# Chunk sums, gate and squares of a Mamba-2 mixer kept in their PSUM banks, the sum of squares moved to VectorE

## The chip, the core and the metric

The kernel runs on one core of a Trainium2 chip: TensorE (PE) for matmuls, VectorE (DVE), ScalarE (ACT) and GpSimd (POOL) for elementwise work, SyncE (SP) for issuing transfers. TensorE writes into PSUM, which has eight banks of 128 partitions x 512 fp32 here; the other engines' data lies in SBUF. The metric is the time of one execution in microseconds on the device. Differences are ratios of times of the kernel before and after on the same chip.

## What is computed

One layer of a diffusion backbone: a bidirectional Mamba-2 mixer over 512 latent tokens, whose scans begin with the state that 256 context tokens leave, and then a convolutional gated MLP. All is fp32 at a model width of 1024, with 32 heads of 64 channels in four groups, states of 128, chunks of 128 tokens. Cut to what matters here:

```python
def ssd_chunked(xs, dt, a, bm, cm, init, with_output):
    ...
    cb = jnp.einsum("bclgn,bcsgn->bcgls", cc, bc)
    mix = cb[:, :, :, None] * jnp.exp(segsum(la))
    y = (jnp.einsum("bcgrls,bcsgrp->bclgrp", mix, xd)
         + jnp.einsum("bclgn,bcgrpn,bcgrl->bclgrp", cc, carried[:, :-1], jnp.exp(la_cs)))

def mamba2_output(y, xs, z, d, norm_w, w_out):
    y = (y.astype(z.dtype) + d * xs).reshape(bsz, l, SSM_INNER)
    return rmsnorm(y * jax.nn.silu(z), norm_w) @ w_out
...
x = x + g1 * ol
x = x + g2 * conv_ffn(modulate(rmsnorm(x, norm2_w[i]), sh2, sc2), ...)
return rmsnorm(x, final_norm_w)
```

`y` is summed over the two directions. For each chunk of a group it has three parts: within the chunk, from the forward state, and from the backward state.

## The kernel before

The features lie in the partitions, the tokens in the free dimension. `u` is an SBUF array of 16 tiles of 128 features x 512 tokens; it holds `xs` at first and is turned into the gated `y` in place. fp32 matmuls are made of three passes: a weight is split by `split` into a high part `hi` (a cast on ScalarE) and a rest `lo` (a subtraction on VectorE, some on GpSimd), and `mm3` adds hi x hi, lo x hi and hi x lo in one bank.

The mixer goes over four groups of heads (`ssm_group`), and within a group over four chunks. For a chunk, `mixing` makes the decay matrices: for each half of the heads and each direction a row `L` is loaded from DRAM, GpSimd writes a diagonal `dg`, VectorE scans `L`; GpSimd adds both directions and multiplies with `cb`. `mixing` also loads `eb`, the decays of the carried states (one buffer, 128 x 2 x 512, two transfers on SP's queue). Then, in lines 760 to 784: TensorE makes `pi`, the part within the chunk, and for each direction `pe`, the part of a carried state `S`. VectorE multiplies each `pe` by its half of `eb`, in SBUF, adds the halves, adds `d * u + pi` into `u` with four instructions on 128 x 128 (those with `d_col`), and adds the sum of the halves into `u`. `pi` and `pe` take turns in the three banks of the pool `py`. `advance` carries a state on: `weighted` (GpSimd's `xw`, ScalarE's `xh`, VectorE's `xl`), three matmuls into `ps_S`, a product on GpSimd and an addition on VectorE.

`gate_pieces` (lines 786 to 801) makes, for each of the 16 feature tiles `m`, the projection `pz` in one of the three banks of the pool `pj`, its Silu `sz` in SBUF on ScalarE, the product `u * sz` on VectorE, the square `sq` in SBUF on ScalarE, and on GpSimd the running sum `acc` of the squares (the first square goes straight into `acc`). `sz` and `sq` take slots of the three-slot SBUF tag `w2k`, which the convolutions `cv` use too. `acc` is later summed over the partitions by TensorE (`ssq`) for the mixer's norm.

`proj_pieces` (projections `pl`, `pc`, convolution and Silu of the next group), `gate_pieces` and `ada_pieces` (sums of the conditioning on VectorE, `ada_acc`) are the fill: `blend` strews it among the pieces of `ssm_group`, the next group's projections beside this group's chunks. That is the order of the program; the order on each engine is made when the program is built, by a scheduler that places instructions by its own reckoning of when buffers and operands come free. On the chip each engine takes its instructions in that order. After the mixer follow the output projection `o` in eight accumulators, three of which take over the banks of `pj`, and the MLP (`pa`, `pg`, `d`).

Nearly every instruction is recorded at line 58, the wrapper of the engines, so the views are read by tiles.

Of the kernel before, what the change touches and what calls it, by code (L numbers as in the profile page):

```python
# [39 lines left out]
# (exp(r) - 1) / r for |r| <= ln(2) / 2, and log(1 + u) / u for 0 <= u <= 1 in powers of u - 1/2  # L40
# [7 lines left out]
class Engine:  # L48
    """an engine whose instructions keep the order of the program while `held` is set"""
# [16 lines left out]
def hybrid_kernel(  # L66
# [21 lines left out]
    # ---------------------------------------------------------------- helpers  # L88
# [50 lines left out]
    def mean_part(p_, n, b):  # L139
        """p_ / n + b"""  # L140
        nb = small.tile([P, 1], F32, tag="rp_b", name="rp_b")
        V.scalar_tensor_tensor(nb, p_, 1.0 / n, eps_c if b is None else b, ALU.mult, ALU.add)
        return nb

    def rsqrt_pair(parts, n, b=None):
        """two factors per partition whose product is 1 / sqrt(sum(parts) / n + EPS); b is a mean_part"""
# [13 lines left out]
    # ---------------------------------------------------------------- constants  # L160
# [51 lines left out]
    # ---------------------------------------------------------------- conditioning  # L212
    def ada_mm(ps, k, w):
        """rows of s @ ada_w, partial sums in the partitions 32 j + (lat, ctx)"""
        j = k % 4
        mm(ps[32 * j:32 * j + 32, :], s_pad[:, k], w, start=(k < 4), stop=(k >= 4))
# [28 lines left out]
    def ada_load(q):  # L245
        """columns [256 q, 256 q + 256) of the shifts and of the scales"""
# [39 lines left out]
    def keep_busy(n, ps=junk):  # L286
        """the clock of the tensor engine falls while it waits"""
# [13 lines left out]
    def normalize(i, eng=V):  # L301
        """token blocks i and i + 1"""
# [45 lines left out]
    def ada_cols(q):  # L348
        """shift and scale of the features [256 q, 256 q + 256), then h there"""
# [20 lines left out]
    # ---------------------------------------------------------------- dt of all heads  # L370
# [8 lines left out]
    def spread(dst, src, eng=V):  # L379
        """heads (g j e) of both directions to the rows (direction, copy, g e j)"""  # L380
# [42 lines left out]
    def first_pair(js, q, vs=(0, 1)):  # L423
        """features [256 q, 256 q + 256) of the tiles js; the low parts of h come last"""
# [157 lines left out]
    def tokcol(tk, dr, ch, g, n=HPG, q=0):  # L582
        """per-token columns of group g's heads; ch 0..3 latent chunks, 4..5 context"""
# [4 lines left out]
    # ---------------------------------------------------------------- mixer  # L588
# [11 lines left out]
    def proj_pieces(g):  # L600
        """a load and the arithmetic on it for each tile of the group, then its context states"""
        def start():
            """the slots are taken when the arithmetic on the group before is in the program"""
# [80 lines left out]
    def ssm_group(g):  # L684
# [75 lines left out]
        for ch in range(NC):  # L760
# [8 lines left out]
            for dr, S in ((0, Sf), (1, Sb[ch])):  # L769
# [3 lines left out]
                V.tensor_tensor(t[:, dr], pe, eb[:, dr], op=ALU.mult)  # L773
            V.tensor_tensor(t[:, 0], t[:, 0], t[:, 1], op=ALU.add)
# [3 lines left out]
            us = u[:, 4 * g:4 * g + 4, cs]  # L778
            V.tensor_tensor(us, us, t[:, 0], op=ALU.add)
# [6 lines left out]
    def gate_pieces(g):  # L786
        def run(raw, m):
            whi, wlo = split(raw, f"z{m}")
            ps = project(whi, wlo, hhi, hlo, LAT, f"pz{m}")
            sz = w2.tile([P, LAT], F32, tag="w2k", name=f"sz{m}")  # L790
            A.activation(sz, ps, AF.Silu)
            V.tensor_tensor(u[:, m], u[:, m], sz, op=ALU.mult)
            if m == 0:
                A.activation(acc, u[:, m], AF.Square)
            else:
                sq = w2.tile([P, LAT], F32, tag="w2k", name=f"sq{m}")
                A.activation(sq, u[:, m], AF.Square)
                G.tensor_tensor(acc, acc, sq, op=ALU.add)
# [7 lines left out]
    # rest of the conditioning: sums over the rows of ada_w in each partition, then over the partitions  # L806
    ada_acc = const.tile([P, D], F32, name="ada_acc")

    def ada_pieces(part, a, spare=False, then=None):
        """sums over k of s_k times row k of the part's columns in each partition"""  # L810
# [42 lines left out]
    def stream(pieces, ahead=2):  # L853
        """the pieces one by one, the loads ahead of the arithmetic"""
# [42 lines left out]
    def blend(main, phase, ratio):  # L897
        """ratio pieces of the fill after each piece of main, then what is left of the phase"""
# [281 lines left out]
```

## Time and profile before

| | us |
|---|---|
| median of three runs | 997.22 (996.68 to 998.53) |
| the profiled execution, first to last instruction (span) | 995.1 |
| TensorE busy | 919.8 |
| VectorE busy | 767.1 |
| GpSimd busy | 419.5 |
| ScalarE busy | 359.3 |

The page gives the profiled execution's own time as its span; the runs' times have what lies around it. Busy times are sums over instructions. A wait is put down to the engine or transfer that came last. A group of instructions is named by what it writes and reads, without buffer numbers, so `eb<-pe,eb` is a product of `pe` and `eb` that is written into `eb`.

### The profile page before, as it was taken

The numbers are of one execution on the slowest core, as the hardware profiler recorded it, in microseconds if no ns is written. First come the engines' busy times: TensorE is split into PE (matmuls) and PEld (weight loads), VectorE is DVE, ScalarE is ACT, GpSimd is POOL, SyncE is SP. The second block draws the span as 40 slices with busy tenths as digits, with TensorE's granted clock in tenths as the row PEclk, the third lists the DMA queues.
The fourth block names the chain that finished last, engine by engine and source line by source line (L and its number), as shares of the span: only waits on it lengthen the run. The fifth ranks groups of instructions, "written<-read, shape, count | busy, mean of one in ns | idle before, by whom it ended". The sixth has DMA issues, their size and how long they took to land.

```text
span 995.1 us, 12394 instructions
## 1 busy us (share of the span) xinstructions
PE 919.8 (92%) x4632; PEld 755.2 (76%) x4632; DVE 767.1 (77%) x1028; ACT 359.3 (36%) x548; POOL 419.5 (42%) x314
## 2 busy tenths in 40 slices
PE   7998879997998888888899999999999999999996
PEld 6687767776787667666788888888878888888885
DVE  4689967999999999978864348778898888843336
ACT  6462334323323232333144334544443433321223
POOL 2133238757886867888720003102300000453446
PEclk9999989999898999999989999999999999999999
DMA  9923363365344554442325360334534233323312
GB/s 299 287 68 109 93 187 114 102 196 170 107 135 130 169 149 130 134 124 66 112 80 190 90 186 1 106 89 144 165 106 130 86 97 94 106 84 91 100 64 84
DMA packets 125028, 123.84 MB, mean 124 GB/s; under 512 B 6029, under 2 KB 101289, under 8 KB 124969
## 3 DMA queue, kind: packets, MB, share of 16 engines
q1 hardware_dynamic: 124969, 123.06, 41.5%
q8 instruction: 36, 0.59, 0.2%
q14 instruction: 23, 0.19, 0.1%
HBM read 120.68 MB, written 2.36 MB: 124 GB/s over the span
## 4 chain that ended last, share of the span: by engine, by line
PE 43%; DVE 7%; issue 1%; ACT 1%; POOL 1%; DMA 0%; DVEq 0%; SPq 0%; POOLq 0%; ACTq 0%
PE d L58 12%; PE pg L58 10%; PE pa L58 10%; PE o L58 8%; PE pz L58 2%; DVE fc L58 1%; DVE xn L58 1%; ACT xn L58 1%; DVE lo_a L58 0%; DMA eb<-e_d 0%; DVE eb L58 0%; DVE flo L58 0%; POOL L L58 0%; DVE u L58 0%; DVE lo_g L58 0%
## 5 line engine op out<-in xcount | busy, mean ns | idle before, releaser
L58 DVE SCALAR_TENSOR_TENSOR fc<-pa,prmC,fc 128x441 f32<-128x441 f32 (+2 forms) x176 | 121.3, 692 | 14.4 <-ACT fc L58 11.0
L58 POOL TENSOR_TENSOR raw_d<-raw_d,g2r 128x1024 f32<-128x1024 f32 x22 | 56.7, 2579 | 179.0 <-DMA raw_d<-in_ffn_w_down_dram 171.3
L58 DVE TENSOR_TENSOR_SCAN L<-L,dg 128x512 f32<-128x512 f32 x64 | 99.7, 1558 | 14.8 <-POOL dg L58 14.0
L58 POOL TENSOR_SCALAR_AFFINE_SELECT dg<-tok_dt 128x512 f32<-128x512 f32 x64 | 64.1, 1001 | 44.6 <-DVE L L58 36.2
L58 PE MATMUL pa<-h2hi,lo_a 128*128 128x512 f32 (+1 forms) x192 | 72.0, 375 | 0.2 <-DVE lo_a L58 0.2
L58 PE MATMUL pa<-h2hi,hi_a 128*128 128x512 f32 (+1 forms) x192 | 71.9, 374 | 0.2 <-ACT h2hi L58 0.2
L58 PE MATMUL pa<-h2lo,hi_a 128*128 128x512 f32 (+1 forms) x192 | 71.3, 371 | 0.8 <-POOL h2lo L58 0.5
L58 PE MATMUL pg<-h2hi,lo_g 128*128 128x512 f32 (+1 forms) x184 | 70.8, 385 | 0.4 <-DVE lo_g L58 0.4
L58 PE MATMUL pg<-h2hi,hi_g 128*128 128x512 f32 (+1 forms) x184 | 70.4, 383 | 0.0
L58 POOL TENSOR_TENSOR L<-L,L 128x512 f32<-128x512 f32 x32 | 50.9, 1592 | 45.1 <-issue 21.1
L58 PE MATMUL pg<-h2lo,hi_g 128*128 128x512 f32 (+1 forms) x184 | 69.7, 379 | 0.0
L58 DVE TENSOR_TENSOR lo_d<-raw_d,hi_d 128x1024 fp32r<-128x1024 f32 x18 | 34.4, 1909 | 44.8 <-ACT hi_d L58 44.8
L58 POOL TENSOR_TENSOR L<-L,cb 128x512 f32<-128x512 f32 x32 | 56.3, 1765 | 0.1
L58 PE MATMUL pz<-hlo,hi_z 128*128 128x512 f32 x128 | 52.3, 408 | 0.0
L58 ACT CAST xh<-xw 128x512 fp32r<-128x512 f32 x40 | 24.7, 617 | 75.7 <-POOL xw L58 70.9
L58 PE MATMUL pz<-hhi,hi_z 128*128 128x512 f32 x128 | 51.8, 405 | 0.0
L58 PE MATMUL pl_x<-hhi,hi_x 128*128 128x512 f32 x128 | 50.9, 399 | 0.7 <-DVE cv_cx L58 0.7
L58 POOL TENSOR_TENSOR g2r<-g2r,adaw 128x1024 f32<-128x1024 f32 x7 | 17.6, 2518 | 80.4 <-issue 52.6
L58 PE MATMUL pz<-hhi,lo_z 128*128 128x512 f32 x128 | 51.1, 399 | 0.0
L58 PE MATMUL pl_x<-hhi,lo_x 128*128 128x512 f32 x128 | 50.9, 399 | 0.0
L58 PE MATMUL pl_x<-hlo,hi_x 128*128 128x512 f32 x128 | 50.4, 395 | 0.0
L58 DVE TENSOR_TENSOR xl<-xw,xh 128x512 fp32r<-128x512 f32 x40 | 43.5, 1088 | 4.4 <-ACT xh L58 4.4
(338 smaller groups left out, 2566.1 us busy)
## 6 DMA issues: line engine op xcount, KB each, us to landing
adaw<-in_ada_w_dram SPq DMA_DIRECT2D x32, 512.0 KB, 3.6
L<-da_d SPq DMA_DIRECT2D x64, 256.0 KB, 4.1
raw_a<-in_ffn_w_up_dram SPq DMA_DIRECT2D x22, 512.0 KB, 4.9
raw_g<-in_ffn_w_up_dram SPq DMA_DIRECT2D x22, 512.0 KB, 4.0
raw_d<-in_ffn_w_down_dram SPq DMA_DIRECT2D x22, 512.0 KB, 3.5
adaw<-in_ada_w_dram SPq DMA_DIRECT2D x8, 1024.0 KB
raw_x<-in_ssm_w_in_dram SPq DMA_DIRECT2D x16, 512.0 KB, 4.1
eb<-e_d SPq DMA_DIRECT2D x32, 256.0 KB, 4.2
```

Source lines behind the costliest of these rows:

```text
L58: ins = f(*a, **kw)
```

## The change

In a chunk, the first direction's product goes into SBUF as before, the second one's back into its own bank `pe`. The sum of both reads one from SBUF and one from PSUM. It is then added to `pi`, in `pi`'s bank, and the four instructions with `d_col` take `pi` with everything in it; the last addition into `u` is gone. In a gate piece, Silu is written back into the projection's bank, `u` is multiplied from there, the square is written into the same bank, and VectorE instead of GpSimd adds it to `acc`.

```diff
                 for j in range(4):
                     mm(pe[:, j], S[:, j * P:(j + 1) * P], cT[:, cs])
-                V.tensor_tensor(t[:, dr], pe, eb[:, dr], op=ALU.mult)
-            V.tensor_tensor(t[:, 0], t[:, 0], t[:, 1], op=ALU.add)
+                V.tensor_tensor(pe if dr else t[:, 0], pe, eb[:, dr], op=ALU.mult)
+
+            V.tensor_tensor(t[:, 0], t[:, 0], pe, op=ALU.add)
+            V.tensor_tensor(pi, pi, t[:, 0], op=ALU.add)
             for j in range(4):
                 us = u[:, 4 * g + j, cs]
                 V.scalar_tensor_tensor(us, us, d_col[:, 4 * g + j:4 * g + j + 1], pi[:, j], ALU.mult, ALU.add)
-            us = u[:, 4 * g:4 * g + 4, cs]
-            V.tensor_tensor(us, us, t[:, 0], op=ALU.add)
...
             ps = project(whi, wlo, hhi, hlo, LAT, f"pz{m}")
-            sz = w2.tile([P, LAT], F32, tag="w2k", name=f"sz{m}")
-            A.activation(sz, ps, AF.Silu)
-            V.tensor_tensor(u[:, m], u[:, m], sz, op=ALU.mult)
+            A.activation(ps, ps, AF.Silu)
+            V.tensor_tensor(u[:, m], u[:, m], ps, op=ALU.mult)
             if m == 0:
                 A.activation(acc, u[:, m], AF.Square)
             else:
-                sq = w2.tile([P, LAT], F32, tag="w2k", name=f"sq{m}")
-                A.activation(sq, u[:, m], AF.Square)
-                G.tensor_tensor(acc, acc, sq, op=ALU.add)
+                A.activation(ps, u[:, m], AF.Square)
+                V.tensor_tensor(acc, acc, ps, op=ALU.add)
```

Comments and docstrings are left out in the changed file, which moves line numbers by two at most.

The scheduler also places other instructions anew, from the first group's chunks up to the first tiles of the output projection. Three places follow. The first is VectorE at the first chunk of the last group (`pe301` is group 3, chunk 0, direction 1; `Sf` and `xl` belong to `advance`, `L` to `mixing`, `lo_z` to a gate's weights); before:

```order
L58 TENSOR_TENSOR eb30_3787<-pe301_3905,eb30_3787 128x512
L58 TENSOR_TENSOR Sf3_1_3954<-Sf3_1_3954,ps_Sf3_1_3944 128x512
L58 TENSOR_TENSOR eb30_3787<-eb30_3787 128x512
L58 TENSOR_TENSOR xl3_1_0_4090<-xw3_1_0_4086,xh3_1_0_4088 128x512
L58 SCALAR_TENSOR_TENSOR u_102<-u_102,d_col_85,pi31_3994 128x128 x4
L58 TENSOR_TENSOR u_102<-u_102,eb30_3787 128x4x128
L58 SCALAR_TENSOR_TENSOR L3300_4125<-L3300_4125,dg3300_4127 128x512
L58 TENSOR_TENSOR u_102<-u_102,sz10_4297 128x512
```

and now:

```order
L58 TENSOR_TENSOR pe301_3894<-pe301_3894,eb30_3780 128x512
L58 TENSOR_TENSOR Sf3_1_3943<-Sf3_1_3943,ps_Sf3_1_3933 128x512
L58 TENSOR_TENSOR eb30_3780<-eb30_3780,pe301_3894 128x512
L58 TENSOR_TENSOR xl3_1_0_4075<-xw3_1_0_4071,xh3_1_0_4073 128x512
L58 TENSOR_TENSOR pi30_3879<-pi30_3879,eb30_3780 128x512
L58 SCALAR_TENSOR_TENSOR u_102<-u_102,d_col_85,pi30_3879 128x128 x4
L58 SCALAR_TENSOR_TENSOR L3300_4110<-L3300_4110,dg3300_4112 128x512
L58 TENSOR_TENSOR u_102<-u_102,pz9_4218 128x512
L58 TENSOR_TENSOR lo_z12_4320<-raw_z12_4247,hi_z12_4319 128x1024
```

The addition into `u` behind the four `d_col` instructions is gone; `pi` gets the sum ahead of them, and they take this chunk's `pi30`, where before they took the next chunk's `pi31`, since they needed no `pe`.

The second is VectorE behind the last chunk (`pi33`), where the last gates' products stand among the splits of weights `lo` and the operands `ul` of the output projection; before:

```order
L58 TENSOR_TENSOR u_102<-u_102,eb33_4149 128x4x128
L58 SCALAR_TENSOR_TENSOR ul2_4568<-u_102,prmA_80,uh2_4567 128x512
L58 SCALAR_TENSOR_TENSOR ul3_4650<-u_102,prmA_80,uh3_4649 128x512
L58 SCALAR_TENSOR_TENSOR ul4_4684<-u_102,prmA_80,uh4_4683 128x512
L58 TENSOR_TENSOR u_102<-u_102,sz12_4371 128x512
L58 TENSOR_TENSOR lo_z15_4450<-raw_z15_4377,hi_z15_4449 128x1024
L58 TENSOR_TENSOR lo_g1b_4522<-ada_acc_832,hi_g1b_4521 128x1024
L58 TENSOR_TENSOR u_102<-u_102,sz13_4408 128x512
```

and now:

```order
L58 SCALAR_TENSOR_TENSOR u_102<-u_102,d_col_85,pi33_4185 128x128 x4
L58 TENSOR_TENSOR lo_z15_4421<-raw_z15_4352,hi_z15_4420 128x1024
L58 TENSOR_TENSOR u_102<-u_102,pz12_4323 128x512
L58 TENSOR_TENSOR u_102<-u_102,pz13_4358 128x512
L58 TENSOR_TENSOR lo_g1b_4491<-ada_acc_832,hi_g1b_4490 128x1024
L58 TENSOR_TENSOR acc_706<-acc_706,pz12_4323 128x512
L58 TENSOR_TENSOR acc_706<-acc_706,pz13_4358 128x512
L58 TENSOR_TENSOR u_102<-u_102,pz14_4391 128x512
L58 TENSOR_TENSOR lo_o0_4513<-raw_o0_4510,hi_o0_4512 128x1024
L58 TENSOR_TENSOR acc_706<-acc_706,pz14_4391 128x512
```

Each gate has two rows now, its product and its addition to `acc`; the addition for `pz12` stands behind the product for `pz13` and a split.

The third is TensorE in the first group, at chunk 1 (`pe010`, `pe011`: forward and backward; `pl_x02`, `pc_x12`: projections of the fill, for group 2; `ps_Sf`: the next state); before:

```order
L58 MATMUL pl_x02_2235<-hlo_288,hi_x02_2206 128x512
L58 MATMUL pe010_1480<-cT0_840,Sf0_1_1402 128x128 x4
L58 MATMUL pe011_1486<-cT0_840,Sb0_1_1319 128x128 x4
L58 MATMUL ps_Sf0_2_1528<-xh0_1_0_1531,bk00_1160 128x512
L58 MATMUL ps_Sf0_2_1528<-xh0_1_0_1531,bk01_1161 128x512
L58 MATMUL ps_Sf0_2_1528<-xl0_1_0_1533,bk00_1160 128x512
L58 MATMUL pi02_1541<-L0200_1498,xk0_1169 64x128 x4
L58 MATMUL pi02_1541<-L0210_1510,xk0_1169 64x128 x4
```

and now, 18 rows behind `pe010`:

```order
L58 MATMUL pc_x12_2400<-chi_104,lo_x12_2397 128x256
L58 MATMUL pc_x12_2400<-clo_289,hi_x12_2396 128x256
L58 MATMUL pe011_1486<-cT0_840,Sb0_1_1319 128x128 x4
L58 MATMUL ps_Sf0_3_1661<-xh0_2_0_1664,bk00_1160 128x512
L58 MATMUL ps_Sf0_3_1661<-xh0_2_0_1664,bk01_1161 128x512
L58 MATMUL pc_x12_2400<-chi_104,hi_x12_2396 128x256
L58 MATMUL ps_Sf0_3_1661<-xl0_2_0_1666,bk00_1160 128x512
L58 MATMUL pc_x12_2400<-chi_104,lo_x12_2397 128x256
```

The two `pe` of the chunk no longer stand together: the second comes 18 projection matmuls later, and `pi02` follows later still, among the matmuls of `pl_x12`.

## Rows read from the trace of the kernel before

**Rows 1.** The page, parts 1 and 2: busy time; busy tenths in 40 slices

```profile
PE 919.8 (92%) x4632; PEld 755.2 (76%) x4632; DVE 767.1 (77%) x1028; ACT 359.3 (36%) x548; POOL 419.5 (42%) x314
...
PE   7998879997998888888899999999999999999996
...
DVE  4689967999999999978864348778898888843336
```

**Rows 2.** Windows: stretch, length; busy of PE, PEld, DVE, ACT, POOL; PEclk; DMA

```profile
150.00:375.00 225.00, 199.90 (x1152) 167.35 (x1151) 214.32 (x253) 73.77 (x124) 167.09 (x124) 0.96 0.48 140
375.00:425.00 50.00, 41.71 (x207) 32.72 (x205) 47.86 (x55) 14.99 (x23) 37.41 (x29) 0.93 0.45 139
425.00:510.00 85.00, 75.09 (x373) 61.14 (x374) 66.17 (x76) 26.02 (x40) 61.05 (x43) 0.94 0.32 95
510.00:531.00 21.00, 21.00 (x97) 17.25 (x96) 10.03 (x12) 10.61 (x15) 7.29 (x4) 1.00 0.42 129
```

**Rows 3.** Groups by form, VectorE, 60 to 530 us, columns as on the page

```profile
L58 DVE TENSOR_TENSOR xl<-xw,xh 128x512 fp32r<-128x512 f32 x40 | 43.5, 1088 | 4.4 <-ACT xh L58 4.4
...
L58 DVE TENSOR_TENSOR eb<-pe,eb 128x512 f32<-128x512 f32 x32 | 20.8, 679 | 10.0 <-DMA eb<-e_d 10.0
L58 DVE SCALAR_TENSOR_TENSOR u<-u,d_col,pi 128x128 f32<-128x128 f32 x64 | 18.0, 335 | 2.3 <-PE pi L58 2.3
L58 DVE TENSOR_TENSOR eb<-eb 128x512 f32<-128x512 f32 x16 | 17.1, 1068 | 0.1
L58 DVE TENSOR_TENSOR u<-u,sz 128x512 f32<-128x512 f32 x16 | 15.1, 945 | 5.1 <-ACT sz L58 5.1
...
L58 DVE TENSOR_TENSOR u<-u,eb 128x512 f32<-128x512 f32 x16 | 14.3, 893 | 0.1
...
L58 DVE SCALAR_TENSOR_TENSOR ul<-u,prmA,uh 128x512 fp32r<-128x512 f32 x5 | 3.5, 744 | 0.0
...
L58 DVE TENSOR_TENSOR lo_g1b<-ada_acc,hi_g1b 128x1024 fp32r<-128x1024 f32 x1 | 1.2, 1212 | 0.0
```

**Rows 4.** Tile `eb`, VectorE: duration ns min/median/max, first and last start

```profile
L58 DVE TENSOR_TENSOR eb<-pe,eb x32: 658/678/693, 164.4 to 505.7; 128x512 f32<-128x512 f32 x32
L58 DVE TENSOR_TENSOR eb<-eb x16: 677/968/1829, 202.4 to 506.4; 128x512 f32<-128x512 f32 x16
```

**Rows 5.** Groups by form, GpSimd, 60 to 530 us: the sum of squares

```profile
L58 POOL TENSOR_TENSOR acc<-acc,sq 128x512 f32<-128x512 f32 x15 | 23.6, 1574 | 21.5 <-ACT sq L58 21.4
```

**Rows 6.** Waits, 60 to 530 us: first VectorE's, then TensorE's; total, times, longest

```profile
DVE L L58 <- POOL dg L58: 14.0, 12, 3.6
DVE eb L58 <- DMA eb<-e_d: 10.0, 7, 4.0
...
PE pe L58 <- DVE eb L58: 4.0, 5, 1.7
...
PE pi L58 <- DVE u L58: 0.6, 1, 0.6
```

**Rows 7.** Chain that ended last, 300 to 532 us: start us, us, what

```profile
474.03 1.75 DVE eb L58
...
479.60 4.77 DMA eb<-e_d
...
493.02 1.60 POOL L L58
...
496.87 1.97 PE pi L58 x8
...
504.03 11.70 PE pz L58 x51
```

**Rows 8.** Timeline, VectorE, 470 to 510 us: start us, us, instruction, [idle before]

```profile
484.49 1.29 DVE L58 TENSOR_TENSOR eb<-pe,eb 128x512 f32<-128x512 f32 x2 [0.96 <-DMA eb<-e_d]
...
496.84 1.29 DVE L58 TENSOR_TENSOR eb<-pe,eb 128x512 f32<-128x512 f32 x2 [1.15 <-DMA eb<-e_d]
...
505.07 1.29 DVE L58 TENSOR_TENSOR eb<-pe,eb 128x512 f32<-128x512 f32 x2 [3.98 <-DMA eb<-e_d]
```

## The prediction

> **What bounds the kernel now.** I read the page's first two parts first. TensorE is busy 92% of the span and VectorE 77%, but the slices (24.9 us each) show two different programs: from 174 to 423 us VectorE stands at 9 tenths without a break, with 7 and 8 up to 498 us, and from there on TensorE does [rows 1]. The change touches only the first of them, so I asked for the busy time by stretches [rows 2]: in 150 to 375 us VectorE is busy 214.32 of 225 us, in 375 to 425 us 47.86 of 50, in 425 to 510 us 66.17 of 85, where GpSimd has 61.05 as well. TensorE idles in all three (25.1 + 8.3 + 9.9 = 43.3 us) and not at all in 510 to 531 us. So up to 510 us the work of VectorE sets the pace, with GpSimd beside it at the end, and what VectorE loses or gains there moves the end of the kernel, up to TensorE's 43 us of idle time. From 531 us on each engine has the same instructions in the same order in both builds, but for the first tiles of the output projection, so nothing else should move.
>
> The chain of waits says the same of the end of that stretch [rows 7]: a chunk's sums on VectorE, then a 4.77 us transfer of the next chunk's factors `eb`, later GpSimd's `L`, then TensorE's `pi` and `pz`.
>
> Then VectorE's instructions by form [rows 3]. Three forms on 128x512 read both operands from SBUF: `eb<-eb` (1068 ns), `u<-u,eb` (893 ns), `u<-u,sz` (945 ns). `eb<-pe,eb`, the same operation and size with one operand from PSUM, takes 679 ns. The tile's view tells how the means come about [rows 4]: the PSUM form lies between 658 and 693 ns in all 32 cases; `eb<-eb` begins at 677 ns and runs up to 1829. So it isn't the memory's speed; some of the SBUF forms are held up, and the PSUM form never is. I read that as waiting for a GpSimd instruction.
>
> **The change part by part.**
>
> (1) *Chunk sums.* VectorE keeps eight instructions a chunk: two products, two sums, four with `d_col`. Both sums now read one operand from PSUM: 16 x (1.068 - 0.679) = 6.2 us and 16 x (0.893 - 0.679) = 3.4 us, together -9.6 us [rows 3]. All 16 chunks lie where VectorE is the bound. Bounds: 0 (the wait goes elsewhere, see 7) and -9.6.
>
> (2) *Gate product.* 16 x (0.945 - 0.679) = 4.3 us; in the order 12 of the 16 stand ahead of the last chunk's end: -3.2 us. The other four fall in TensorE's stretch and are worth nothing.
>
> (3) *Sum of squares.* 15 additions come to VectorE at 0.679 us, 10.2 us. In the order 11 of them stand ahead of the last chunk's end: +7.5 us. Four fall in 510 to 531 us, where VectorE is busy 10.03 of 21 us [rows 2], and TensorE's matmuls cover them.
>
> (4) *GpSimd* loses those 15 additions of 1.574 us, 23.6 us [rows 5]. 11 of them (17.3 us) lie in 375 to 510 us, among 37.4 + 61.1 = 98.5 us of its work there [rows 2]. VectorE waits 14.0 us for GpSimd's `dg` in all [rows 6]; 17.3 / 98.5 of that is -2.5 us. Bounds: 0 and -17.3, if GpSimd were the bound there.
>
> (5) *The slot of `eb`.* There is one buffer. It used to come free behind the chunk's addition into `u`, which mostly stands behind the four `d_col` instructions; now it does behind the addition into `pi`, ahead of them. Those four take 4 x 0.335 = 1.3 us [rows 3]. VectorE waits 10.0 us in 7 places for that transfer [rows 6], the longest 3.98 us in the last chunk [rows 8]. 7 x 1.3 = 9.1 us is the most, 0 the least; waits shorter than that, and rows that moved in between, leave about half: -4 us.
>
> (6) *Banks are held longer*, the price of the change. `pi` used to be free after its four `d_col` instructions, which needed nothing of `pe`; now both products and two sums come first. The second `pe` is held over one more instruction. A gate's bank (one of three) used to be free after Silu; now Silu, product, square and addition have to be done, and the addition stands in VectorE's queue behind other work and waits there for ScalarE's square, with the scans and splits behind it. TensorE runs in order, so a late bank stops the projections behind it. Of such waits the trace has 4.0 us (`pe` for `eb`) and 0.6 us (`pi` for `u`) today [rows 6]. The tail is the likeliest place: `pz15` needs the bank of `pz12`, whose addition stands behind the last `pe`'s product and sum, the addition into `pi`, five `ul`, four `d_col`, two gate products and two splits. With 0.68 us for a 512-column instruction, 0.74 for `ul`, 1.2 for a split [rows 3] that is 0.68 x 6 + 0.74 x 5 + 1.3 + 1.2 x 2 = 11.5 us and some waits; TensorE has 53 matmuls from the last `pe` to `pz15`, 53 x 11.70 / 51 = 12.2 us [rows 7]. So nothing to 3 us there. Bounds for all banks: 0 and two instructions a chunk, 16 x 2 x 0.68 = 21.8 us. I take +3 us, near the 4.6 us that such waits cost now.
>
> (7) *Stretch that comes back.* VectorE's next instruction with two SBUF operands may meet the same GpSimd instruction that the sum used to wait for; `xl` has the same shape and takes 1088 ns [rows 3]. Between none and all of 9.6 + 3.2 = 12.8 us; I take a quarter, +3.2 us, since what follows often reads PSUM.
>
> (8) *Writing PSUM.* VectorE writes no PSUM in the trace. The nearest row is `eb<-pe,eb`; I take its 0.679 us. 0.1 us either way for 32 such instructions is 3.2 us. ScalarE's 31 writes into PSUM lie on an engine that is busy 36% [rows 1] and cost nothing.
>
> [...]
>
> Sum: -9.6 - 3.2 + 7.5 - 2.5 - 4.0 + 3.0 + 3.2 = -5.6 us. On the profiled span of 995.1 us that is 989.5. The median of the three runs, 997.2, lies 2.1 us above that span, so the forecast is **991.5 us**, by itself 985 to 995.
>
> **The rivals.**
>
> *A. GpSimd gives more.* If GpSimd is the bound from 375 to 510 us, its 17.3 us count whole in place of 2.5: 991.5 - 14.8 = 977. For it: VectorE idles 18.8 us in 425 to 510 us, and the chain goes through GpSimd's `L` [rows 2, 7]. Against it: VectorE takes the same additions over, and it is at 47.86 of 50 us before. [...]
>
> *B. The waits only move.* All 12.8 us come back on `xl`, scans and splits, in place of 3.2: 991.5 + 9.6 = 1001; 996 if the eight additions that GpSimd starts in 425 to 510 us today (8 x 0.679 = 5.4 us) go into VectorE's idle time there. For it: `xl` at 1088 ns. Against it: the PSUM forms that follow.
>
> *C. Slower: the banks.* TensorE comes to the next chunk's `pi` before VectorE has freed a bank. For it: the new order puts the two `pe` of a chunk up to 18 matmuls apart, and `pi` later among the projections. If the two sums stand in TensorE's way in every chunk, 21.8 us in place of 3: 991.5 + 18.8 = 1010; in half of the chunks 1001. It decides when VectorE takes longer from a chunk's first product to its last `d_col` than the chunk's period lets it: some 8 us of instructions by the order, in a period of 496.84 - 484.49 = 12.4 us [rows 8]. Against it: these 4 us to spare.
>
> *D. The PSUM forms don't do it*: 0.1 us longer each, for the 63 instructions with the new forms, +6.3 us: 998, and 995 by half.
>
> **How the numbers follow.** Forecast 0.52, A 0.14, B 0.12, C 0.16, D 0.06. A measurement of this kernel can tell about 0.2% (2 us) from no change. Faster by more: the forecast but for its edge (0.50), A, half of D: 0.67. Slower: C and a third of B, 0.20. Within: 0.13. The range runs from A's 977 to the lower half of C, 1003; the upper half of C and what lies below A stay out.
>
> **What would show it.** VectorE's sums and gate products between 650 and 750 ns with no long ones: (1), (2), (8) are right. GpSimd's busy time lower by 20 to 30 us and VectorE's by 2 to 10: (3), (4). VectorE's waits for `eb`'s transfer at 3 to 7 us: (5). TensorE's waits for VectorE before `pe`, `pi` and `pz` under 8 us: (6); past 20 us, C is the case. If `xl`, the scans and `lo_z` grow by what the sums lose, (7) was too low and B holds. From 531 us on all lengths must stay; if they don't, the prediction looked at the wrong place.

## The result, and the profile after

The changed kernel takes 981.29 us (median of four runs, 980.93 to 984.91) beside 996.95 us before (median of four, 996.54 to 998.53): a ratio of 0.985, with a 95% interval of 0.9831 to 0.987. The forecast was a gain of 5.6 us, as a time 991.5 us; the profiled span fell by 15.5 us, from 995.1 to 979.6. The direction was right and the time lies in the range, but the gain is nearly three times the forecast, and about a third of it comes from the step that I had put down as a loss.

The page after, parts 1 and 2, answers to [rows 1]:

```profile
PE 915.8 (93%) x4632; PEld 753.1 (77%) x4632; DVE 756.6 (77%) x1043; ACT 358.8 (37%) x548; POOL 382.8 (39%) x299
...
PE   7999779898989988899999999999999999999996
...
DVE  4689968899899999889954457877998888843336
```

VectorE is busy 10.5 us less, although it has 15 instructions more, and GpSimd 36.7 us less, though the 15 additions that it lost took 23.6 [rows 5].

The windows after (columns as in [rows 2]), and then the stretch from 60 us to the last chunk's last `d_col` instruction, first after and then before, where it ended with the last addition into `u`:

```profile
150.00:375.00 225.00, 201.73 (x1164) 169.78 (x1163) 209.12 (x251) 76.30 (x127) 157.55 (x122) 0.95 0.47 140
375.00:425.00 50.00, 44.28 (x220) 35.52 (x220) 44.51 (x63) 13.93 (x22) 34.04 (x28) 0.90 0.50 142
425.00:510.00 85.00, 81.64 (x418) 65.48 (x417) 72.90 (x95) 34.28 (x51) 45.27 (x34) 1.00 0.40 121
...
60.00:493.51 433.51, 389.62 (x2159) 325.06 (x2158) 393.41 (x522) 151.16 (x246) 267.86 (x210) 0.95 0.46 134
```

```profile
60.00:509.00 449.00, 393.40 (x2153) 327.46 (x2153) 404.71 (x508) 151.23 (x246) 296.04 (x221) 0.95 0.44 129
```

The mixer's last sum comes 15.5 us earlier (509.0 to 493.5 us), as much as the span fell. For VectorE the two lines split it: its work fell by 11.3 us (404.7 to 393.4) and its idle time by 4.2 (44.3 to 40.1). From the start of the output projection to the end it is 473.8 us before (from 521.3) and 474.8 after (from 504.8): nothing is gained behind the mixer.

The chain of waits that ended last, after, 470 to 516 us (start, us, what), answers to [rows 7]:

```profile
470.15 1.60 DVE L L58
471.75 0.59 DVE eb L58
...
472.48 1.13 PE pe L58 x8
...
478.98 1.55 PE pi L58 x16
...
486.89 12.15 PE pz L58 x53
...
505.01 0.69 PE o L58 x3
...
```

From 472 us to the end of this stretch the chain is TensorE alone, but for 0.1 us. Before, it went through VectorE's sums, `eb`'s transfer and GpSimd's `L` up to 497 us.

VectorE's groups by form after, 60 to 530 us, answer to [rows 3]; two rows of before that weren't shown follow:

```profile
L58 DVE TENSOR_TENSOR_SCAN L<-L,dg 128x512 f32<-128x512 f32 x64 | 101.7, 1590 | 19.9 <-POOL dg L58 17.3 <-DMA L<-da_d 2.4
L58 DVE TENSOR_TENSOR xl<-xw,xh 128x512 fp32r<-128x512 f32 x40 | 37.6, 939 | 1.5 <-ACT xh L58 1.5
...
L58 DVE TENSOR_TENSOR lo_z<-raw_z,hi_z 128x1024 fp32r<-128x1024 f32 x16 | 25.5, 1592 | 0.0
...
L58 DVE TENSOR_TENSOR pi<-pi,eb 128x512 f32<-128x512 f32 x16 | 11.0, 688 | 0.1
L58 DVE TENSOR_TENSOR pe<-pe,eb 128x512 f32<-128x512 f32 x16 | 10.9, 684 | 0.0
L58 DVE TENSOR_TENSOR eb<-pe,eb 128x512 f32<-128x512 f32 x16 | 10.8, 678 | 4.4 <-DMA eb<-e_d 4.4
L58 DVE TENSOR_TENSOR u<-u,pz 128x512 f32<-128x512 f32 x16 | 10.8, 677 | 4.7 <-ACT pz L58 4.5
L58 DVE TENSOR_TENSOR eb<-eb,pe 128x512 f32<-128x512 f32 x16 | 10.7, 670 | 0.1
...
L58 DVE TENSOR_TENSOR acc<-acc,pz 128x512 f32<-128x512 f32 x15 | 10.1, 675 | 0.1
```

```profile
L58 DVE TENSOR_TENSOR_SCAN L<-L,dg 128x512 f32<-128x512 f32 x64 | 99.7, 1558 | 14.8 <-POOL dg L58 14.0 <-issue 0.4
...
L58 DVE TENSOR_TENSOR lo_z<-raw_z,hi_z 128x1024 fp32r<-128x1024 f32 x16 | 27.6, 1724 | 0.1
```

The five forms that are new take 670 to 688 ns. And `xl` and `lo_z`, which the change doesn't touch, got shorter: 43.5 to 37.6 us and 27.6 to 25.5 us.

Why instructions that nobody edited get shorter can be seen in the trace of before, 468 to 477 us, VectorE's rows and then GpSimd's (start us, us, instruction):

```profile
468.64 1.15 DVE L58 TENSOR_TENSOR xl<-xw,xh 128x512 fp32r<-128x512 f32 x1
469.72 1.11 DVE L58 TENSOR_TENSOR u<-u,sz 128x512 f32<-128x512 f32 x1
470.75 2.08 DVE L58 TENSOR_TENSOR lo_z<-raw_z,hi_z 128x1024 fp32r<-128x1024 f32 x1
...
473.95 1.83 DVE L58 TENSOR_TENSOR eb<-eb 128x512 f32<-128x512 f32 x1
```

```profile
469.20 1.09 POOL L58 TENSOR_SCALAR_AFFINE_SELECT dg<-tok_dt 128x512 f32<-128x512 f32 x1
470.26 1.49 POOL L58 TENSOR_TENSOR xw<-xk,tok_w 128x512 f32<-128x512 f32 x1
471.71 2.26 POOL L58 TENSOR_TENSOR L<-L,cb 128x512 f32<-128x512 f32 x1
473.93 1.30 POOL L58 TENSOR_TENSOR acc<-acc,sq 128x512 f32<-128x512 f32 x1
```

In these rows they take turns. `eb<-eb` starts beside `acc`, which ends at 475.23, and ends 0.55 us behind it (475.78); its shortest case takes 0.68 us. `u<-u,sz` ends 0.54 us behind `dg`, with 0.66 us for its shortest. It goes the other way too: `L<-L,cb` starts at 471.71 beside `lo_z`, which ends at 472.83, and ends 1.14 us behind that; its shortest case takes 1.26 us. So in these rows an instruction with two SBUF operands on VectorE and one on GpSimd that meet don't run side by side: the later one ends about as far behind the other as it takes by itself.

### The profile page after: what moved, and what is told of

It is laid out like the page before. It is cut to its first block, busy times and chain, and to the rows that moved or that the text cites. A ratio compares the mean times of both kernels' runs of the same rounds, so it can differ in the third digit from the quotient of the medians.

```text
span 979.6 us, 12391 instructions
## 1 busy us (share of the span) xinstructions
PE 915.8 (93%) x4632; PEld 753.1 (77%) x4632; DVE 756.6 (77%) x1043; ACT 358.8 (37%) x548; POOL 382.8 (39%) x299
## 4 chain that ended last, share of the span: by engine, by line
PE 38%; issue 6%; DVE 6%; DMA 2%; ACT 1%; POOL 1%; DVEq 0%; SPq 0%; ACTq 0%
PE d L58 12%; PE o L58 8%; PE pg L58 7%; PE pa L58 7%; PE pz L58 3%; DVE fc L58 1%; DMA adaw<-in_ada_w_dram 1%; POOL g2r L58 1%; DVE xn L58 1%; DVE lo_a L58 1%; PE pe L58 1%; ACT xn L58 0%; DMA L<-da_d 0%; DVE flo L58 0%; DVE xl L58 0%
## 5 line engine op out<-in xcount | busy, mean ns | idle before, releaser
L58 DVE SCALAR_TENSOR_TENSOR fc<-pa,prmC,fc 128x441 f32<-128x441 f32 (+2 forms) x176 | 121.3, 693 | 14.6 <-ACT fc L58 11.2
L58 DVE TENSOR_TENSOR_SCAN L<-L,dg 128x512 f32<-128x512 f32 x64 | 101.7, 1590 | 19.9 <-POOL dg L58 17.3
L58 POOL TENSOR_SCALAR_AFFINE_SELECT dg<-tok_dt 128x512 f32<-128x512 f32 x64 | 61.9, 967 | 38.6 <-DVE L L58 29.9
L58 POOL TENSOR_TENSOR L<-L,L 128x512 f32<-128x512 f32 x32 | 46.0, 1436 | 55.4 <-issue 26.6
L58 POOL TENSOR_TENSOR L<-L,cb 128x512 f32<-128x512 f32 x32 | 56.6, 1774 | 1.3 <-ACT cb L58 1.2
L58 POOL TENSOR_TENSOR x<-x,ot 128x512 f32<-128x512 f32 x4 | 5.2, 1292 | 107.8 <-DVE ot L58 105.4
```

The lines of the kernel that those rows point to most:

```text
L58: ins = f(*a, **kw)
```

## The experiments

A table first; the ratio is to the kernel before, measured beside it on the same chip, and the microseconds are (ratio - 1) x 997. An interval is 1.3 to 3.4 us to either side, mostly 2, so two rows that differ by less than 3 us, with the widest intervals less than 4, can't be told apart.

| kernel | ratio, 95% interval | us to before |
|---|---|---|
| the change | 0.985, 0.9831 to 0.987 | -15.0 |
| chunk sums alone (`e_sums`) | 0.9954, 0.994 to 0.9967 | -4.6 |
| sum of squares alone (`e_accv`) | 0.995, 0.9934 to 0.9967 | -5.0 |
| gate product and sum of squares (`e_gate`) | 0.9888, 0.9864 to 0.9912 | -11.2 |
| the change without the sum of squares (`e_accpool`) | 0.9902, 0.9883 to 0.992 | -9.8 |
| sum of squares on VectorE from SBUF (`e_accv_sb`) | 0.9947, 0.9929 to 0.9965 | -5.3 |
| a fourth slot, nothing else (`e_slot`) | 0.9994, 0.9977 to 1.001 | -0.6 |
| the change + GpSimd additions (`e_dummy`) | 0.9894, 0.9868 to 0.9919 | -10.6 |
| the change + VectorE additions (`e_vdummy`) | 0.9849, 0.9826 to 0.9872 | -15.1 |
| the change + one-column additions (`e_gtiny`) | 0.9929, 0.9907 to 0.9951 | -7.1 |
| before, other order (`e_ratio_b`) | 1.0015, 1.0002 to 1.0028 | +1.5 |
| the change, other order (`e_ratio_a`) | 0.9841, 0.9813 to 0.987 | -15.9 |
| the change, products added one by one (`e_each`) | 0.9876, 0.985 to 0.9902 | -12.4 |
| the change + state products on VectorE (`e_sfv`) | 0.9882, 0.9851 to 0.9912 | -11.8 |
| the change + context products, PSUM (`e_xwc`) | 0.9934, 0.9914 to 0.9955 | -6.6 |
| the change + context products, SBUF (`e_xwc_sb`) | 0.99, 0.9866 to 0.9934 | -10.0 |

**The parts apart.** Chunk sums alone: the kernel before with the first half of the diff. What was expected:

> Only the chunk part of the change: second product into its bank, both sums with one operand from PSUM; gate and sum of squares as in the kernel before. Theory L (the gain is VectorE's own shorter instructions, each part by its own lengths): the 32 sums lose 9.7 us, the product into PSUM costs 0.2, so about 987.5 (985 to 990), the two-SBUF instructions that are left (xl, scans, lo_z) as long as before. Theory P (pairs: a VectorE instruction with two SBUF operands and a GpSimd instruction stretch each other, so each pair that goes away shortens others too): more than the sums' own, 981 to 986, with xl shorter by 3 us or more in all and GpSimd's instructions beside acc shorter by 8 us or more. Theory O (the gain is the order that the scheduler happened to find): no fixed relation, 975 to 1000.

The gate part alone: the kernel before with the second half of the diff.

> Only the gate part of the change: Silu and square in the gate's bank, product and sum of squares on VectorE with one operand from PSUM; chunk sums as before. Theory L: the products give 3.7 us, the additions cost 7.4, so slower by about 4: 998 to 1002. Theory P, with GpSimd as a bound from 375 us on: GpSimd loses 16 us of its work there and VectorE's other instructions get shorter: faster by 4 to 9 us, 988 to 993. Theory O: 980 to 1005, with no relation to the parts.

The change, with the squares back in SBUF and their sum on GpSimd:

```diff
-                A.activation(ps, u[:, m], AF.Square)
-                V.tensor_tensor(acc, acc, ps, op=ALU.add)
+                sq = w2.tile([P, LAT], F32, tag="w2k", name=f"sq{m}")
+                A.activation(sq, u[:, m], AF.Square)
+                G.tensor_tensor(acc, acc, sq, op=ALU.add)
```

> The changed kernel with the sum of squares left on GpSimd (squares in an SBUF slot as before); chunk sums and gate product from PSUM as changed. Theory L: VectorE has 7.4 us less work than in the changed kernel, so faster than it: 974 to 980. Theory P with GpSimd as a bound: GpSimd has 16 us more in 355 to 495 us: slower than the changed kernel by 4 to 9 us, 985 to 990, and TensorE waits for L again (5 us or more). Theory O: 970 to 995.

The kernel before with that edit the other way round and nothing else:

> The kernel before with the sum of squares alone moved: the square goes into the gate's bank and VectorE adds it; chunk sums and gate product as before. Theory L: 7.4 us of work come to VectorE: 1000 to 1005. Theory P with GpSimd as a bound: GpSimd's 16 us there count for more than VectorE's 7.4: 990 to 996. Theory O: 980 to 1005.

The parts add up. The sum of squares gives 5.0 us on the kernel before and 5.2 as the last step (-9.8 to -15.0). The gate product gives 6.2 on top of it (-5.0 to -11.2) and 5.2 beside the chunk sums (-4.6 to -9.8). The chunk sums give 4.6 alone and 3.8 last. So theory L falls with the sum of squares, which it had as a loss of 3 to 8 us. Theory P has its time right for the sum of squares (991.0 and 986.5 us), has too little for the gate part (984.4 where it had 988 to 993), and one of its signs failed: TensorE's waits for `L` in `e_accpool` are 2.7 us, not 5 or more. For the chunk sums its time is wrong: they gave less than their own lengths (991.7 us), not more, though both of its signs came (`xl` 3.7 us shorter, GpSimd 9.3 us less busy). VectorE's busy time bears on this; the page, part 1, of the chunk sums alone, and three of its groups on VectorE:

```profile
PE 912.9 (92%) x4632; PEld 750.6 (76%) x4632; DVE 766.0 (78%) x1028; ACT 359.4 (36%) x548; POOL 410.2 (42%) x314
```

```profile
L58 DVE TENSOR_TENSOR_SCAN L<-L,dg 128x512 f32<-128x512 f32 x64 | 106.3, 1661 | 20.0 <-POOL dg L58 14.2 <-DMA L<-da_d 3.9 <-PE pl_x L58 1.3
...
L58 DVE TENSOR_TENSOR lo_z<-raw_z,hi_z 128x1024 fp32r<-128x1024 f32 x16 | 28.8, 1801 | 0.0
L58 DVE TENSOR_TENSOR u<-u,sz 128x512 f32<-128x512 f32 x16 | 19.2, 1201 | 5.7 <-ACT sz L58 5.5
```

The sums are 9.7 us shorter, but VectorE as a whole only 1.1 us (767.1 to 766.0): the scans take 6.6 us more than before, the gate products 4.1, `lo_z` 1.2, while `xl` takes 3.7 us less and the sums `ada_acc` about 2. By these rows, most of what the sums no longer wait, other instructions with two SBUF operands do. That is the prediction's rival B, in this part, though on other instructions than `xl`.

The sum of squares alone, the page and the same groups with `eb<-eb`:

```profile
PE 918.4 (93%) x4632; PEld 754.3 (76%) x4632; DVE 768.9 (78%) x1043; ACT 358.3 (36%) x548; POOL 394.7 (40%) x299
```

```profile
L58 DVE TENSOR_TENSOR_SCAN L<-L,dg 128x512 f32<-128x512 f32 x64 | 99.8, 1559 | 13.5 <-POOL dg L58 12.7 <-issue 0.3
...
L58 DVE TENSOR_TENSOR lo_z<-raw_z,hi_z 128x1024 fp32r<-128x1024 f32 x16 | 26.1, 1631 | 0.0
...
L58 DVE TENSOR_TENSOR eb<-eb 128x512 f32<-128x512 f32 x16 | 15.0, 935 | 0.1
...
L58 DVE TENSOR_TENSOR u<-u,sz 128x512 f32<-128x512 f32 x16 | 13.1, 816 | 5.6 <-ACT sz L58 5.5
```

VectorE takes over 10.1 us of additions and is busy only 1.8 us more: `eb<-eb` gives back 2.1 us, `u<-u,sz` 2.0, `lo_z` 1.5. GpSimd is busy 24.8 us less. The window up to the mixer's last sum, to be laid beside the one of before:

```profile
60.00:502.88 442.88, 395.47 (x2173) 329.61 (x2172) 405.33 (x520) 152.34 (x248) 278.51 (x210) 0.95 0.45 131
```

The sum comes 6.1 us earlier. VectorE's work is the same as before there (405.3 and 404.7 us), although 11 of the additions are in it, and its idle time falls from 44.3 to 37.6.

**Slots, and the operand from PSUM.** Two other reasons why the gate part might pay. The kernel before with `bufs=4` in place of 3 for the pool of `w2k`:

> The kernel before with four in place of three SBUF slots for the rows that the convolutions, Silu and the squares share; all instructions as before. Theory S: a good part of the 12 us that the gate part gave comes from slots that come free late: 986 to 992. Theory P: the slots held nothing up that matters: 994 to 998.

The kernel before with `G` changed to `V` in the line that adds `sq` to `acc`:

> The kernel before with the additions of the squares moved from GpSimd to VectorE and nothing else: the squares stay in their SBUF slot, so VectorE reads two operands from SBUF. Theory P: GpSimd gets its 16 us, VectorE's other two-SBUF instructions get shorter by some 8 us, and the additions take 0.75 to 1.1 us in place of 0.68: 991 to 994, a little worse than with the square in PSUM (991.0). If the place of the square decides (slots, or the PSUM operand): 996 to 1002.

The slot gives nothing (-0.6 us, the interval spans 1). The additions from SBUF give as much as from PSUM (5.3 and 5.0), although they take 1040 ns each in place of 676. So for the sum of squares it is the engine that it left that counts; neither the slot nor the operand shows.

**What an engine's time costs.** Additions that nobody reads, behind each addition to `acc` in the changed kernel, on GpSimd and on VectorE (`spare` is an SBUF row of its own, cleared at the start):

```diff
                 V.tensor_tensor(acc, acc, ps, op=ALU.add)
+                G.tensor_tensor(spare, spare, u[:, m], op=ALU.add)
```

> The changed kernel with 15 more additions on GpSimd (a spare row plus u of the gate, 128x512, both operands in SBUF) that nobody reads. Nothing waits for them and no slot or bank hangs on them, so only GpSimd's time and its company with VectorE are added. Theory P (what the sum of squares cost on GpSimd was GpSimd's time and the stretch of VectorE's two-SBUF instructions): GpSimd 20 to 25 us busier, VectorE 6 to 11 us busier with the same instructions, the time back up by 4 to 7 us: 985 to 988. Theory S (the gain came from the SBUF slots that sz and sq no longer take): unchanged, 980 to 983.

```diff
                 V.tensor_tensor(acc, acc, ps, op=ALU.add)
+                V.tensor_tensor(spare, spare, ps, op=ALU.add)
```

> The changed kernel with 15 more additions on VectorE of the form of the sum of squares (a spare row plus the gate's bank, one operand from PSUM) that nobody reads: 10.1 us of work, about 7.4 us of it ahead of the last chunk's end, and the gate's bank is held by one instruction more. If VectorE is the bound from 355 to 495 us: 7 us or more slower, 988 to 991. If VectorE and GpSimd share the bound there, about two thirds: 985 to 987. If GpSimd alone sets the pace: 981 to 983.

On GpSimd they cost 4.4 us, on VectorE nothing that shows (-15.1 beside -15.0; by medians 987.5 and 983.2 beside 981.3, that is 6.2 and 1.9). These two ran on the same chip, and their times lie 2.2 us or more apart. VectorE's additions are not quite free in the mixer: in the profiled run its last sum comes 5.6 us later (499.1 us), but the output projection now begins ahead of some gates and the span is only 2.3 us longer. With GpSimd's additions VectorE is busy 768.4 us, 11.8 more than in the changed kernel with the same instructions, and GpSimd 407.0, 24.2 more. The page, part 1, and VectorE's scans of that run:

```profile
PE 913.5 (93%) x4632; PEld 750.8 (76%) x4632; DVE 768.4 (78%) x1043; ACT 358.1 (36%) x548; POOL 407.0 (41%) x315
```

```profile
L58 DVE TENSOR_TENSOR_SCAN L<-L,dg 128x512 f32<-128x512 f32 x64 | 108.7, 1699 | 19.3 <-POOL dg L58 16.6 <-PE pl_x L58 1.3 <-DMA L<-da_d 0.7
```

To part GpSimd's time from the stretch, 12 additions of one column in place of each of these:

```diff
                 V.tensor_tensor(acc, acc, ps, op=ALU.add)
+                for _ in range(12):
+                    G.tensor_tensor(spare[:, :1], spare[:, :1], u[:, m, :1], op=ALU.add)
```

> The changed kernel with 12 additions of one column (128x1) on GpSimd for each of 15 gates, which nobody reads: GpSimd's time without the traffic of the 15 additions of 512 columns. If GpSimd's time is what the additions of 512 columns cost: the time goes up by 0.28 us for each us that GpSimd gets, as in the run with those additions (6.2 us for 22.5): with 15 to 25 us of GpSimd's time 985 to 988, VectorE's busy time as in the changed kernel. If the stretch of VectorE's instructions is the cost: 980 to 983, and VectorE's busy time within 3 us of 756.6.

```profile
PE 910.1 (92%) x4632; PEld 746.9 (76%) x4632; DVE 752.6 (76%) x1043; ACT 358.4 (36%) x548; POOL 437.7 (44%) x480
```

```profile
L58 DVE TENSOR_TENSOR_SCAN L<-L,dg 128x512 f32<-128x512 f32 x64 | 99.4, 1553 | 31.1 <-POOL dg L58 23.8 <-POOL spare L58 4.5 <-DMA L<-da_d 1.8
```

They were slower than I had thought and gave GpSimd 54.9 us more, and at 989.8 us the time lies above both expectations. VectorE is not stretched (752.6 us); instead its scans wait 28.3 us for GpSimd (17.3 in the changed kernel), and the time is up by 7.9 us. That is 0.14 us for each us of GpSimd, half of what I expected and not nothing. The windows up to the mixer's last sum, with the wide additions and with those of one column, tell how each costs its time:

```profile
60.00:503.54 443.54, 390.56 (x2165) 325.42 (x2164) 404.00 (x523) 152.44 (x248) 284.07 (x221) 0.96 0.45 132
...
60.00:500.85 440.85, 381.97 (x2148) 317.12 (x2147) 390.97 (x522) 150.95 (x246) 307.53 (x342) 0.97 0.46 131
```

In the changed kernel VectorE is busy 393.4 us and idle 40.1 up to there. With the wide additions the sum comes 10.0 us later (the span is 6.7 us longer), and VectorE's busy time has grown by 10.6 us and its idle time not at all (39.5); its scans don't wait longer for `dg` either (16.6 us, 17.3 in the changed kernel). With those of one column it comes 7.3 us later, with 9.8 us more idle time and 2.4 us less work. So in these two traces GpSimd's time costs in two ways, by stretching VectorE's instructions and by letting VectorE wait for `dg`; the wide additions show the first and those of one column the second, and the rate of the one doesn't price the other. Taking the sum of squares away from GpSimd gave both: idle time in `e_accv`, and mostly work as the last step (VectorE's work up to the last sum is 397.8 us in `e_accpool`, 4.4 more than in the changed kernel, which has the additions on VectorE besides).

**The order.** Every edit makes the scheduler place other instructions anew, so the gain might be an order that happened to be good. The four numbers that spread the fill, in both kernels:

```diff
-    for g, ratio in enumerate((0.6, 0.6, 0.9, 0.6)):
+    for g, ratio in enumerate((0.7, 0.7, 0.8, 0.7)):
```

> The kernel before with the numbers that spread projections and gates over the chunks changed from 0.6, 0.6, 0.9, 0.6 to 0.7, 0.7, 0.8, 0.7: the same instructions in another order, so that the gain can be read under a second order. Theory P: whatever this order costs by itself, the changed kernel with the same numbers is faster by 11 to 19 us. Theory O: the two come within 6 us of each other.

> The changed kernel with the same other numbers, 0.7, 0.7, 0.8, 0.7. Theory P: 11 to 19 us below the kernel before with these numbers. Theory O: within 6 us of it.

Under this order the change is worth 17.4 us (+1.5 to -15.9), under the first one 15.0. Theory O falls for the change as a whole; its parts were not measured under this order.

**Banks.** The changed kernel with each product in SBUF and added to `pi` by itself:

```diff
-                V.tensor_tensor(pe if dr else t[:, 0], pe, eb[:, dr], op=ALU.mult)
-
-            V.tensor_tensor(t[:, 0], t[:, 0], pe, op=ALU.add)
-            V.tensor_tensor(pi, pi, t[:, 0], op=ALU.add)
+                V.tensor_tensor(t[:, dr], pe, eb[:, dr], op=ALU.mult)
+                V.tensor_tensor(pi, pi, t[:, dr], op=ALU.add)
```

> The changed kernel with each product added to the chunk's bank by itself: the second product goes into SBUF, not into its bank, and the two sums are both additions of an SBUF row to the bank. As many VectorE instructions, one operand from PSUM each; the second pe is free one instruction sooner, its product is not written to PSUM. If holding the banks costs something today (my 3 us): 978 to 980. If it costs nothing: 980 to 983. If the order makes the difference: 970 to 992.

Freeing `pe` sooner gains nothing (2.6 us the other way, within what can be told). The banks are not all that differs: VectorE's waits for `eb`'s transfer are 9.4 us here, 4.4 in the changed kernel. TensorE's waits for VectorE that can be for a bank, in the changed kernel, 60 to 530 us:

```profile
PE tx L58 <- DVE eb L58: 3.5, 2, 2.2
...
PE pe L58 <- DVE u L58: 2.9, 2, 1.8
PE pe L58 <- DVE eb L58: 2.7, 4, 1.1
...
PE pi L58 <- DVE eb L58: 0.9, 1, 0.9
```

**More off GpSimd.** If GpSimd's time is dear, more of its work might go. Its products of the state with the decay, for the last two groups:

```diff
-            G.tensor_tensor(heads(n), heads(S), ej(etb[:, dr, hs, ch]), op=ALU.mult)
+            (V if g > 1 else G).tensor_tensor(heads(n), heads(S), ej(etb[:, dr, hs, ch]), op=ALU.mult)
```

> The changed kernel with the 12 products of the state with its decay (128x512, both operands from SBUF) of the last two groups on VectorE in place of GpSimd. Theory P, GpSimd the dearer engine behind 355 us: GpSimd loses 12 x 1.4 = 17 us, VectorE gets 12 x 0.8 = 10 us: faster by 2 to 5 us, 976 to 979. If VectorE is the bound as I forecast: 5 us or more slower, 986 to 992.

Its products `xw` of the context's rows (`weighted` takes the engine as a new argument), once with VectorE reading the transposed rows in their bank, and once reading ScalarE's copy in SBUF:

```diff
-        xk = []
-        for cc in range(2):
-            tp = bank(pt, f"txc{g}{cc}")
...
-            t = cx.tile([P, 512], F32, tag=f"xkc{cc}", name=f"xkc{g}{cc}")
-            A.copy(t, tp)
-            xk.append(t)
         for dr in range(2):
             ps = bank(pst, f"sc{g}{dr}")
             for cc in range(2):
-                local_state(ps, bk, cc, weighted(xk[cc], dr, 4 + cc, g), cc == 0, cc == 1)
+                tp = bank(pt, f"txc{g}{dr}{cc}")
...
+                local_state(ps, bk, cc, weighted(tp, dr, 4 + cc, g, V), cc == 0, cc == 1)
...
```

> The changed kernel with the 16 products of the context's rows and weights on VectorE in place of GpSimd, one operand from PSUM: VectorE reads the transposed rows in their bank, which are transposed once for each direction, and ScalarE's copies of them go away. GpSimd loses 19 us, VectorE gets 16 x 0.69 = 11 us, TensorE 32 transposes of 128 columns. If what decides is that no pair of two-SBUF instructions is left there: as with the sum of squares, 3 to 6 us faster, 975 to 978. If VectorE's time decides in those places (most lie ahead of 375 us, where VectorE is busy 9 tenths): 983 to 988.

> The changed kernel with the same 16 products on VectorE, both operands from SBUF as GpSimd reads them; nothing else moved. If the operand from PSUM decides: 3 us or more above the run that reads PSUM, its products between 0.7 and 1.2 us. If only the engine decides: within 2 us of it.

None pays: 3.2 (within what can be told), 8.4 and 5.0 us worse than the change, and no expectation was met: the state products lie between the two theories, the products from PSUM are the slowest and those from SBUF in between. From PSUM the products do take 674 ns in place of 875, and VectorE (754.3 us) and GpSimd (356.0) are both less busy than in the changed kernel. TensorE's waits in it:

```profile
PE pe L58 <- DVE u L58: 10.3, 5, 4.2
...
PE tb L58 <- DVE xw L58: 4.9, 3, 3.0
PE txc L58 <- DVE xw L58: 4.4, 4, 1.7
```

The pool `pt` has one bank. Held until VectorE has come to the product, it stops TensorE before the next transposes (`tb`, `txc`), 9.3 us in all. These are waits of the kind of the prediction's rival C, in a place where the change doesn't go. How much of the 8.4 us is theirs isn't shown: this kernel also has 32 transposes more, and TensorE waits 10.3 us for `u` before `pe` (2.9 in the changed kernel). Why the products with two SBUF operands lose too was not tried out; they stand in a chain (`xw`, `xh`, `xl`, state) on which TensorE waits, which the sum of squares doesn't.

## Why the prediction was half right

By the parts that the runs measured, and with the terms for banks and stretch shared out among them by me after the result, the forecast was -9.2 for the chunk sums (9.6 and 4.0 gained, 2.0 given back at the banks, 2.4 as stretch), -2.4 for the gate product (3.2 gained, 0.8 given back) and +6.0 for the sum of squares (7.5 - 2.5 + 1.0). Measured, as means of the two ways in which each was taken, were -4.2, -5.7 and -5.1. So the chunk sums, from which most of the forecast gain came, gave 5 us less than forecast, and the gate part some 14 us more. That the direction came out right and the time within the range is partly luck: the two misses have opposite signs.

- **(1), (2), (8), the new forms' lengths**: right. 670 to 688 ns, 0.679 taken. A write into PSUM cost VectorE at most 0.01 us (684 beside 678 ns).
- **(3) and (4), the sum of squares, is the step that failed.** I put VectorE's additions at their length, +7.5 us, because I read 9 tenths busy as the bound up to 510 us, and GpSimd's at their share of VectorE's waits for `dg`, -2.5; measured was a gain of 5.1 us. Ten more us on VectorE cost 0 to 2 us (`e_vdummy`), 22.5 on GpSimd 4.4 to 6.2 (`e_dummy`). Busy time on VectorE is partly waiting for GpSimd's turn (`eb<-eb` at 473.95 us took 1.83 us beside `acc`, its shortest case 0.68), so its 9 tenths did not show the bound. And (4) priced the wrong wait: VectorE's waits for `dg` fell only from 14.0 to 12.7 us with the sum of squares alone, and they are 17.3 in the changed kernel. What (4) has no term for is that VectorE's own instructions get shorter (10.1 us of additions, 1.8 us more busy in `e_accv`), and that TensorE itself waits for GpSimd's `L`. Those waits, 60 to 530 us, before, with the sum of squares alone, and after the change:

```profile
PE pi L58 <- POOL L L58: 10.3, 9, 2.6
...
PE pi L58 <- POOL L L58: 5.6, 7, 2.0
...
PE pi L58 <- POOL L L58: 1.0, 1, 1.0
```

The 4.7 us between the first two are near the 5.0 us that this part gave alone, but no run changes this wait by itself. In the whole change the chunk sums bear on it too: alone they leave 3.2 us of it, and 4.0 us of waiting for `eb` in its place. How the gain is shared between this wait and the stretch stays open. GpSimd's busy time fell by 36.7 us where I had set 20 to 30, VectorE's by 10.5 where I had set 2 to 10. Rival A had it right that GpSimd gives more, but counting its 17.3 us whole (977) was too much.
- **(5), `eb`'s slot**: right by the waits, 10.0 us in 7 places before [rows 6], 4.4 in 3 after. In the runs without the new chunk sums they are 8.1 to 11.2 us, in those with them at most 5.0, but for the 9.4 of `e_each`, which is at most a little slower than the change. So these waits don't count whole; their share of the time was not measured apart.
- **(6), banks**: 3 us taken. The waits of TensorE for VectorE before `pe` and `pi` went from 4.8 us (4.6 of it in [rows 6]) to 6.5, 3.5 more appeared before the transposes `tx` (one in four takes a bank of `py`), and no wait in the tail. `e_each` gains nothing by an earlier bank. The price is small, as taken; with a one-bank pool (`e_xwc`) such waits came to 9.3 us.
- **(7), the stretch that comes back**: 3.2 us taken of 12.8, one value for the whole. For the chunk sums alone it is much more (VectorE gets 1.1 of 9.7 us), and this is the second term that was mis-sized. With GpSimd's additions gone it turns round: `xl`, `lo_z` and `ada_acc` fall by 5.9, 2.1 and 0.8 us, the scans rise by 2.0. I had let the stretch move between VectorE's instructions and forgotten that its source moves too: the 15 additions were one of the things that it waits for.
- **The gate product** gives 5.7 us, its own lengths 4.3; the difference is within what can be told, but I had taken only 2.4 in all. The page of `e_gate` against that of `e_accv` has VectorE 5.0 us and GpSimd 6.0 us less busy, so here too both engines may gain from the pair that goes away. It was not tried out further.
- **Rival C's half** is added up wrong: 10.9 us in place of 3 make 999 us, not 1001. The measured time lies on the other side of the forecast, so nothing here hangs on it.
- **From 531 us on** little changed, as expected: from the output projection's start to the end it is 1.0 us more.

## What to carry to other kernels

Where VectorE and GpSimd work side by side, look at the spread of a two-SBUF form's durations (`eb<-eb` 677 to 1829 ns here) and lay VectorE's rows beside GpSimd's: a busy share that held such waits, VectorE's 9 tenths, didn't show the bound here, and shortening some of the waiting instructions moved part of the wait to others (with the chunk sums alone 9.7 us less in the sums, 1.1 us less on VectorE). A lower busy share didn't make work cheaper here either: the same 15 additions cost 0 to 2 us on VectorE, busy 77%, and 4 to 6 on GpSimd, busy 39%. Price such work by adding as much again on either engine. It doesn't follow that everything should leave GpSimd: three other moves gained nothing here. An operand in PSUM cost VectorE nothing here (670 to 688 ns, where the shortest form with both operands in SBUF takes some 660 to 680), but look at how many banks its pool has before it stays there: with a pool of one, in `e_xwc`, TensorE waited 9.3 us before the next transposes.

## What was not expected of the hardware

Some of GpSimd's instructions that the edit left alone got quicker as well: `L<-L,L` from 1592 to 1436 ns and `xw<-xkc` from 1343 to 1175, 23.6 us of additions taken away and 36.7 us gone; others did not (`L<-L,cb` 1765 and 1774 ns). An addition of one column on GpSimd takes 184 ns at the least and up to 1162. And a granted clock of 1.00 in place of 0.94 in 425 to 510 us went with TensorE's shorter idle time there (85 - 81.64 = 3.4 us, 9.9 before). But in 375 to 425 us it fell from 0.93 to 0.90 while TensorE's idle time fell as well, from 8.3 to 5.7 us, and over whole profiled runs it did not go with the time: `e_gtiny` had 0.985 as a mean at 989.6 us, the kernel before 0.976 and the changed one 0.974.
